# Two layers of a gated hybrid backbone: first tiles, linear attention and mLSTM reordered for TensorE's neighbours, and attention's logits in runs of four

## The chip, the cores and the metric

The kernel runs on one core of a Trainium2 chip. The metric is the device time of one execution in microseconds (us). The kernel before was run three times: 2300.45, 2302.86 and 2303.84 us, so its median is 2302.86. Engines are named as the profile names them: PE is TensorE (PEld its weight loads), DVE is VectorE, ACT is ScalarE, POOL is GpSimd and SP is SyncE.

## What is computed

There are 256 latent tokens and 256 context tokens of width 1024, and two layers. Every sub-layer is an RMS norm with a shift, scale and gate that a conditioning vector sets.

```python
def trunk_layer(x, ctx, c, c_ctx, cos, sin, lp, last):
    ...
    x = x + 0.5 * mod_l[:, 2] * swiglu(adaln(x, mod_l, 0, g[0]), lp['ffn1_w13'], lp['ffn1_w2'])
    ...
    y_l, y_c = token_mixer(adaln(x, mod_l, 1, g[1]), adaln(ctx, mod_c, 1, g[1]), cos, sin, lp, not last)
    x = x + mod_l[:, 5] * y_l
    x = x + 0.5 * mod_l[:, 8] * swiglu(adaln(x, mod_l, 2, g[2]), lp['ffn2_w13'], lp['ffn2_w2'])
```

The token mixer runs three branches over one input projection: windowed attention (8 query heads, 2 key heads of 64 channels, RMS norms of queries and keys, rope for latent tokens, a sink in the softmax; context tokens see context only, latent ones a window and the context), a bidirectional gated linear attention (4 heads, keys 64 wide, values 128) and a bidirectional mLSTM (4 heads of 128). Each branch is multiplied by a sigmoid gate (`s_a`, `s_g`, `s_m`) of the projection and by an output matrix; the sum goes through `w_o`. The last layer gives latent tokens only.

## The kernel before, in words

**Layout and dense products.** Activations are held with channels on the 128 partitions and tokens along the free axis: 512 columns in layer 0, context first. In layer 1's mixer, queries and what follows from them are needed for the 256 latent tokens alone (`c0=256`), keys and values for all. Every large product is split into a high and a low part: `mm3` (L258 to L260) issues three matmuls per 128x128 block of weights (hi with hi, lo with hi, hi with lo), so a dense tile of 128 channels is 24 matmuls into one PSUM tile of the pool `acc`. Weights come by DMA as `raw`; ACT makes the high part (L224, 128x1024), DVE the low one (L225). These dense matmuls are most of what PE does.

**PSUM and order.** PSUM has two pools of four tiles, `acc` for dense tiles and `mx` for everything else. The program is written in one order; a scheduler of the framework turns it into one instruction list per engine, and each engine takes its list strictly in order. A tile of a pool is given out in program order.

**The start** (`start`). The eight tiles of `x` come by DMA; ACT squares them, and PE sums the squares of the first five over the channels with `ones_d` (L356, through the helper line L340), DVE adds the other three (L361) and PE sums that. `partial(k)` is the product of the conditioning vector with block k of the modulation weights (L401), `vectors(k)` turns it into columns, `norm(k)` applies norm, scale and shift to channel block k (L628 to L630: `t`, `xh`, `xl`), and `unit(u, k)` is the three matmuls of dense tile u with block k. The order here is written out by hand and kept with `seq`.

**Linear attention** (`gla`, twice per layer, `ft` 0 and 1). Each call makes gate sums on ACT and DVE, transposes decayed keys (`t` of L782, PE L785), forms chunk states (L795) and attention within chunks. `fill()` issues the next half of a dense tile of `gr`, or a part of `mv`; there are 16 such steps in a layer, and calls beyond that do nothing.

**mLSTM** (`mlstm`, twice per layer for two heads each). `bcast` (L957 to L961) spreads one row of a table over all partitions: a 128x128 matmul with a one-hot column of `sel`, once for the high and once for the low part. It is called for two directions and two heads, three times each. `den1` (L1017) and `qn` (L1023, L1025) collect the denominators in bands of 32 columns. `head_norm` (L727) closes each head.

**Attention.** Keys and four query tiles go through `qk_norm` (L1062 to L1070): a copy, a square on ACT, a sum over 64 channels on PE (L1067), Ln, Exp and a square on ACT (L575, L576, L578), three steps on DVE; the tables of ACT are loaded anew after each first square (L143). `rope` (L1072 to L1079) turns the latent columns. `attention` then loops over two halves `a` and the blocks of 128 queries: `weights` makes four logit tiles (L1123, 64 channels deep, `kv` 0 and 1 on the two halves of the rows), mask, maximum, exponential and sum; `fills()` issues one dense tile (two in layer 1) of the gate `sa`, of which there are eight; then `values` of the step before transposes the weights in blocks of 128 keys (L1147) and multiplies them with the values (L1154, 64 columns wide).

## Time and profile before

| | |
|---|---|
| median of three runs | 2302.86 us |
| the profiled execution | 2299.65 us |
| its span | 2297.5 us |
| mean granted clock of PE | 0.998 |
| PE busy | 2269.5 us, 99% |
| DVE, ACT busy | 1532.1 us (67%), 970.8 us (42%) |
| DMA | 314.94 MB, mean 137 GB/s |

The 2.15 us between span and time are launch and end. A busy share is a mean over stages; PE's waits stand as single entries in a list, with the instruction that ended each. The stages lie as follows (us from the span's start): start to 57, first FFN of layer 0 to 427, its linear attention to 575, a stretch of dense work to 610, mLSTM to 735, attention with its norms to 862, branches and output to 1003, second FFN to 1365; the same for layer 1 with the first FFN to 1743, linear attention to 1853, mLSTM to 1957, norms to 1988, attention to 2040, output to 2100, and the last FFN to the end.

### The profile page before, as it was taken

The numbers are of one execution on the slowest core, as the hardware profiler recorded it, in microseconds if no ns is written. First come the engines' busy times: TensorE is split into PE (matmuls) and PEld (weight loads), VectorE is DVE, ScalarE is ACT, GpSimd is POOL, SyncE is SP. The second block draws the span as 40 slices with busy tenths as digits, with TensorE's granted clock in tenths as the row PEclk, the third lists the DMA queues.
The fourth block names the chain that finished last, engine by engine and source line by source line (L and its number), as shares of the span: only waits on it lengthen the run. The fifth ranks groups of instructions, "written<-read, shape, count | busy, mean of one in ns | idle before, by whom it ended". The sixth has DMA issues, their size and how long they took to land.

```text
span 2297.5 us, 32871 instructions
## 1 busy us (share of the span) xinstructions
PE 2269.5 (99%) x12494; PEld 1890.6 (82%) x12494; DVE 1532.1 (67%) x3214; ACT 970.8 (42%) x1566; POOL 53.7 (2%) x65
## 2 busy tenths in 40 slices
PE   8999999999999999999999999999999999999999
PEld 4888888877877668888888898888888788889999
DVE  5786875689766763768733357855547897876755
ACT  4322224556545642352222253222246665745443
POOL 0000001000000000200000010000010000001000
PEclk9999999999999999999999999999999999999999
DMA  7655554221212113435532236655433333335764
GB/s 281 220 199 162 193 179 143 92 60 56 83 55 66 63 46 92 156 120 189 172 116 92 83 117 207 200 162 193 152 124 96 90 113 98 125 118 190 233 199 147
DMA packets 140430, 314.94 MB, mean 137 GB/s; under 512 B 30192, under 2 KB 41328, under 8 KB 140144
## 3 DMA queue, kind: packets, MB, share of 16 engines
q1 hardware_dynamic: 139248, 309.69, 41.7%
q0 software_dynamic: 1024, 3.15, 0.4%
q8 instruction: 98, 1.61, 0.3%
q14 instruction: 60, 0.49, 0.1%
HBM read 308.59 MB, written 4.19 MB: 136 GB/s over the span
## 4 chain that ended last, share of the span: by engine, by line
PE 72%; DVE 4%; ACT 2%; DMA 1%; issue 1%; SPq 0%; DVEq 0%; ACTq 0%
PE acc L258 21%; PE acc L259 21%; PE acc L260 20%; PE mx L1123 1%; PE mx L1154 1%; PE mx L1147 1%; DVE lo L225 1%; DMA f<-in_modt_dram 1%; PE mx L1057 1%; PE mx L814 1%; PE mx L988 1%; PE mx L727 1%; PE mx L960 0%; PE mx L1017 0%; PE acc L302 0%
## 5 line engine op out<-in xcount | busy, mean ns | idle before, releaser
L224 ACT CAST hi<-raw 128x1024 fp32r<-128x1024 f32 (+2 forms) x445 | 433.8, 977 | 962.9 <-PE acc L259 623.2
L258 PE MATMUL acc<-xh,hi 128*128 128x512 f32 (+1 forms) x2184 | 779.9, 357 | 5.6 <-ACT xh L629 5.3
L259 PE MATMUL acc<-xl,hi 128*128 128x512 f32 (+1 forms) x2184 | 779.2, 357 | 0.2
L260 PE MATMUL acc<-xh,lo 128*128 128x512 f32 (+1 forms) x2184 | 776.0, 355 | 0.6 <-DVE lo L225 0.6
L225 DVE TENSOR_TENSOR lo<-raw,hi 128x1024 fp32r<-128x1024 f32 (+2 forms) x445 | 502.5, 1132 | 311.1 <-ACT hi L224 302.5
L258 PEld LDWEIGHTS acc<-xh,hi 128*128 128x128 f32 x2184 | 413.5, 189 | 70.8 <-issue 7.0
L259 PEld LDWEIGHTS acc<-xl,hi 128*128 128x128 f32 x2184 | 413.5, 189 | 64.7 <-issue 8.0
L260 PEld LDWEIGHTS acc<-xh,lo 128*128 128x128 f32 x2184 | 413.6, 189 | 62.9 <-issue 5.8
L260 PE MATMUL acc<-f,lo 128*128 128x512 f32 (+1 forms) x896 | 313.7, 350 | 0.0
L258 PE MATMUL acc<-f,hi 128*128 128x512 f32 (+1 forms) x896 | 313.4, 350 | 0.0
L514 DVE SCALAR_TENSOR_TENSOR u<-f,f 128x512 f32<-128x512 f32 x448 | 284.7, 686 | 14.0 <-DMA f<-in_modt_dram 14.0
L259 PE MATMUL acc<-t,hi 128*128 128x512 f32 (+1 forms) x704 | 248.2, 353 | 0.0
L258 PEld LDWEIGHTS acc<-f,hi 128*128 128x128 f32 x896 | 169.4, 189 | 23.2 <-issue 1.2
L260 PEld LDWEIGHTS acc<-f,lo 128*128 128x128 f32 x896 | 169.5, 189 | 22.1 <-issue 0.4
L650 DVE TENSOR_TENSOR t<-t,acc 128x512 f32<-128x512 f32 (+1 forms) x89 | 54.2, 609 | 151.5 <-PE acc L260 150.1
L259 PEld LDWEIGHTS acc<-t,hi 128*128 128x128 f32 x704 | 133.1, 189 | 18.2
L638 DVE SCALAR_TENSOR_TENSOR x<-acc,ggt,x 128x256 f32<-128x256 f32 x136 | 61.2, 480 | 88.1 <-PE acc L260 87.9
L592 POOL TENSOR_TENSOR t<-t,t 128x256 f32<-128x256 f32 x45 | 44.8, 1013 | 1121.4 <-ACT t L588 1121.4
L259 PE MATMUL acc<-x,hi 128*128 128x512 f32 (+1 forms) x192 | 65.3, 342 | 0.0
L314 ACT CAST f<-t 128x512 fp32r<-128x512 f32 (+1 forms) x92 | 51.5, 559 | 20.9 <-DVE t L650 19.2
L629 ACT ACTIVATE xh<-t,mod 128x256 fp32r<-128x256 f32 x88 | 39.3, 500 | 44.2 <-DVE t L628 44.2
L315 DVE TENSOR_TENSOR t<-t,f 128x512 fp32r<-128x512 f32 (+1 forms) x90 | 54.7, 607 | 2.4 <-ACT f L314 2.4
(311 smaller groups left out, 2464.6 us busy)
## 6 DMA issues: line engine op xcount, KB each, us to landing
raw<-in_w_dram SPq DMA_DIRECT2D x179, 512.0 KB, 3.6
f<-in_modt_dram SPq DMA_DIRECT2D x256, 256.0 KB, 4.7
raw<-in_win_dram SPq DMA_DIRECT2D x110, 512.0 KB, 3.5
raw<-in_w_dram SPq DMA_DIRECT2D x61, 384.0 KB, 3.1
raw<-in_w_dram SPq DMA_DIRECT2D x61, 320.0 KB, 2.8
raw<-in_wout_dram SPq DMA_DIRECT2D x16, 512.0 KB, 3.5
raw<-in_wo_dram SPq DMA_DIRECT2D x16, 512.0 KB, 4.0
f<-in_modw_dram SPq DMA_DIRECT2D x16, 256.0 KB, 6.2
```

Source lines behind the costliest of these rows:

```text
L224: a = A.copy(hi[:, :n], raw[:, :n])
L225: b = V.tensor_tensor(lo[:, :n], raw[:, :n], hi[:, :n].bitcast(F32), ALU.subtract)
L258: mm(o, wh, xh[:, cs], start=first, stop=False)
L259: mm(o, wh, xl[:, cs], start=False, stop=False)
L260: mm(o, wl, xh[:, cs], start=False, stop=last)
L314: A.copy(hi[:, cs], src[:, cs])
L315: tt(lo[:, cs], src[:, cs], hi[:, cs].bitcast(F32), ALU.subtract)
L514: V.scalar_tensor_tensor(junk[:], raw[:], 1.0, cond[s][h][:], ALU.mult, ALU.mult, accum_out=part[:, k, s, h:h + 1])
L592: G.tensor_tensor(sums[c.start][0][:, c], sums[c.start][0][:, c], q[:, c], ALU.add)
L629: a = act(xh[:, c], t[:, c], AF.Identity, bias=sh[:, k, s:s + 1])
L638: V.scalar_tensor_tensor(X[m][:, c], ps[:, c], gate[:, m, s:s + 1], X[m][:, c], ALU.mult, ALU.add)
L650: tt(t[:, c], t[:, c], pb[:, c], ALU.mult)
```

## The change

`start`: PE sums all eight squares. The second modulation product stands ahead of the first unit, the second norm and the third product come earlier among the units.

`gla`: one call of `fill()` is added for `ft == 0`, ahead of the loop that forms the decayed keys.

`bcast`: two directions are spread in one call, each with a matmul of 32 rows by 128 columns at its own band of rows, first both high parts, then both low ones. The callers' loops follow, and the four `den1` are written ahead of `qn`.

`attention.weights`: the four logits are written ahead of the softmax, the two of `b=0` in pool `mx`, the two of `b=1` in pool `acc`. `attention.values`: the product of a key block is written behind the transposes of the next one.

```diff
@@ start
             i = seq("ACT", act(q[:], X[k][:], AF.Square))
-            if k < 5:
-                pe(ms[:], ones_d[:], q[:], k == 0, False)
-            elif k == 5:
-                total = q
-            else:
-                tt(total[:], total[:], q[:], ALU.add)
-        pe(ms[:], ones_d[:], total[:], False, True)
+            pe(ms[:], ones_d[:], q[:], k == 0, k == KD - 1)
...
+        partial(1)
         unit(0, 0)
-        partial(1)
-        unit(1, 0)
         vectors(1)
         norm(1)
+        unit(1, 0)
+        partial(2)
         unit(0, 1)
-        partial(2)
+        vectors(2)
         unit(1, 1)
-        vectors(2)
         cast(2, 0)
         norm(2)
@@ gla
         act(ends[:, 2:4, :], ends[:, 0:2, :], AF.Exp, scale=1.0 / 16)
+        if ft == 0:
+            fill()
@@ bcast
-    def bcast(r, hi, lo, cs):
-        ps = mx()
-        s = sel[:, r:r + 1].to_broadcast([128, 128])
-        mm(ps[:, cs], s, hi[:, cs], True, False)
-        mm(ps[:, cs], s, lo[:, cs], False, True)
-        return ps
+    def bcast(rs, hi, lo, cs):
+        out = [mx() for _ in rs]
+        for n, x in enumerate((hi, lo)):
+            for ps, r in zip(out, rs):
+                rows = slice(32 * (r // 2), 32 * (r // 2) + 32)
+                mm(ps[:, cs], sel[rows, r:r + 1].to_broadcast([32, 128]), x[rows, cs], n == 0, n == 1)
+        return out
@@ mlstm
-            for d in range(2):
-                r = 2 * (2 * d + hl) + hp
-                ab = bcast(r, R["ah"], R["al"], cs)
+            for d, ab in enumerate(bcast([2 * (2 * d + hl) + hp for d in range(2)], R["ah"], R["al"], cs)):
...
                 mm(den1[rr, cs], onec[:] if hp == 0 else onec2[:], sw[d, hl][:, cs], True, True)
+        for hl in range(2):
+            for d in range(2):
+                q = 2 * d + hl
+                rr = slice(32 * q, 32 * q + 32)
                 for c in range(q0, 4):
...
-            for d in range(2):
-                r = 2 * (2 * d + hl) + hp
-                rb = bcast(r, rh, rl, cs)
+            rs = [2 * (2 * d + hl) + hp for d in range(2)]
+            for d, rb in enumerate(bcast(rs, rh, rl, cs)):
                 tt(sw[d, hl][:, cs], sw[d, hl][:, cs], rb[:, cs], ALU.mult)
-                wb = bcast(r, wh, wl, cs)
+            for wb in bcast(rs, wh, wl, cs):
                 e = W()
@@ attention.weights
+            pss = {}
             for b in range(2):
                 for kv in range(2):
-                    h, j = 4 * kv + 2 * a + b, 2 * kv + b
                     r = slice(64 * kv, 64 * kv + 64)
-                    ps = mx()
+                    ps = pss[b, kv] = (mx, acc)[b]()
                     mm(ps[:, 0:nk], aq[2 * a + b][r, qc], kh[r, 0:nk], True, True)
+            for b in range(2):
+                for kv in range(2):
+                    h, j, ps = 4 * kv + 2 * a + b, 2 * kv + b, pss[b, kv]
                     if lat:
@@ attention.values
             po = mx()
+            def product(kb, t):
+                for kv in range(2):
+                    mm(po[64 * kv:64 * kv + 64, 0:256], vt[:, kb * 128 + 64 * kv:kb * 128 + 64 * kv + 64],
+                       t[:, 256 * kv:256 * kv + 256], kb == 0, kb == nb - 1)
+            due = None
             for kb in range(nb):
...
-                for kv in range(2):
-                    mm(po[64 * kv:64 * kv + 64, 0:256], vt[:, kb * 128 + 64 * kv:kb * 128 + 64 * kv + 64],
-                       t[:, 256 * kv:256 * kv + 256], kb == 0, kb == nb - 1)
+                if due:
+                    product(*due)
+                due = kb, t
+            product(*due)
```

The order of instructions moves in more places than the diff names. Three of them, on PE; `mx` and `acc` are PSUM tiles, the first number is the tile's.

The start, from the three spare matmuls with `ones_d` on: `acc57` and `acc58` are the first two dense tiles, `mx68` is the second modulation product. Before:

```order
L340 MATMUL acc2_123<-u3_124,ones_d_97 128x512 x2
L340 MATMUL mx63_254<-ct_93,u62_246 128x2 x2
L340 MATMUL acc2_123<-u3_124,ones_d_97 128x512
L340 MATMUL acc57_233<-xh41_217,f36_201 128x512
L340 MATMUL acc57_233<-xh41_217,f37_202 128x512
L340 MATMUL acc57_233<-xl42_218,f36_201 128x512
L401 MATMUL mx68_275<-y26_181,ccs_96 32x256 x2
L401 MATMUL mx68_275<-y27_182,ccs_96 32x256 x2
L401 MATMUL mx68_275<-y28_183,ccs_96 32x256 x2
L401 MATMUL mx68_275<-y29_184,ccs_96 32x256 x2
L340 MATMUL acc58_234<-xh41_217,f64_260 128x512
L340 MATMUL acc58_234<-xh41_217,f65_261 128x512
```

After:

```order
L340 MATMUL acc2_123<-u3_124,ones_d_97 128x512 x2
L340 MATMUL mx63_254<-ct_93,u62_246 128x2 x2
L340 MATMUL acc2_123<-u3_124,ones_d_97 128x512
L395 MATMUL mx68_272<-y26_181,ccs_96 32x256 x2
L395 MATMUL mx68_272<-y27_182,ccs_96 32x256 x2
L395 MATMUL mx68_272<-y28_183,ccs_96 32x256 x2
L395 MATMUL mx68_272<-y29_184,ccs_96 32x256 x2
L340 MATMUL acc57_233<-xh41_217,f36_201 128x512
L340 MATMUL acc57_233<-xh41_217,f37_202 128x512
L340 MATMUL acc57_233<-xl42_218,f36_201 128x512
L340 MATMUL mx70_286<-ct_93,u69_281 128x2 x2
L340 MATMUL acc58_234<-xh41_217,f64_260 128x512
```

The four matmul pairs of `mx68` stand ahead of the first unit in place of behind it, and the second unit (`acc58`) behind `mx70`, the vectors of the second block.

A step of layer 0's attention: L1123 and L1122 are logits, L1147 and L1156 transposes, L1154 and L1149 products with the values. Before, with dense matmuls between the step's first four transposes and these rows:

```order
L1154 MATMUL mx1468_6790<-t1470_6796,f1372_6397 64x256 x2
L1147 MATMUL mx1471_6800<-ct_93,t1440_6661 128x128
L1147 MATMUL mx1471_6800<-ct_93,t1444_6673 128x128
L1147 MATMUL mx1471_6800<-ct_93,t1442_6667 128x128
L1147 MATMUL mx1471_6800<-ct_93,t1446_6679 128x128
L1123 MATMUL mx1476_6814<-f1373_6399,f1382_6446 128x512
L1154 MATMUL mx1468_6790<-t1472_6805,f1372_6397 64x256 x2
L1123 MATMUL mx1478_6821<-f1373_6399,f1382_6446 128x512
L1123 MATMUL mx1480_6828<-f1373_6399,f1391_6493 128x512
L1123 MATMUL mx1482_6835<-f1373_6399,f1391_6493 128x512
L259 MATMUL acc1488_6857<-xl806_3393,hi1486_6853 128x512
```

After:

```order
L1156 MATMUL mx1469_6791<-ct_93,t1446_6679 128x128
L1156 MATMUL mx1471_6798<-ct_93,t1443_6667 128x128
L1156 MATMUL mx1471_6798<-ct_93,t1445_6675 128x128
L1156 MATMUL mx1471_6798<-ct_93,t1444_6671 128x128
L1156 MATMUL mx1471_6798<-ct_93,t1446_6679 128x128
L1122 MATMUL acc1478_6818<-f1373_6399,f1391_6493 128x512
L1122 MATMUL acc1479_6820<-f1373_6399,f1391_6493 128x512
L1149 MATMUL mx1468_6790<-t1470_6796,f1372_6397 64x256 x2
L1149 MATMUL mx1468_6790<-t1472_6803,f1372_6397 64x256 x2
L1122 MATMUL mx1476_6814<-f1373_6399,f1382_6446 128x512
L1122 MATMUL mx1477_6816<-f1373_6399,f1382_6446 128x512
L258 MATMUL acc1488_6857<-xh795_3382,hi1486_6853 128x512
```

One and three logits with a product between have become two and two, with both products between them; the eight transposes stand in one run.

Layer 1's last query norm to the first logits: L1067 and L1066 are the sum over channels of a norm, L1075 and L1074 the rope, `acc3707` the fourth of the eight `sa` gate tiles, `acc3681` the first. Before:

```order
L258 MATMUL acc3707_17614<-xh3025_14294,hi3705_17610 128x256
L259 MATMUL acc3707_17614<-xl3026_14295,hi3705_17610 128x256
L260 MATMUL acc3707_17614<-xh3025_14294,lo3706_17611 128x256
L1067 MATMUL mx3641_17368<-t3640_17364,ct_93 128x256
L1075 MATMUL mx3652_17394<-f3603_17175,ct_93 128x256
L1075 MATMUL mx3654_17400<-f3612_17222,ct_93 128x256
L1075 MATMUL mx3656_17406<-f3621_17269,ct_93 128x256
L258 MATMUL acc3707_17614<-xh3027_14296,hi3705_17610 128x256
L259 MATMUL acc3707_17614<-xl3028_14297,hi3705_17610 128x256
L260 MATMUL acc3707_17614<-xh3027_14296,lo3706_17611 128x256
L258 MATMUL acc3707_17614<-xh3029_14298,hi3705_17610 128x256
```

After:

```order
L1066 MATMUL mx3641_17368<-t3640_17364,ct_93 128x256
L1074 MATMUL mx3652_17394<-f3603_17175,ct_93 128x256
L1074 MATMUL mx3654_17400<-f3612_17222,ct_93 128x256
L1074 MATMUL mx3656_17406<-f3621_17269,ct_93 128x256
L1074 MATMUL mx3658_17412<-f3630_17316,ct_93 128x256
L1074 MATMUL mx3660_17418<-f3639_17363,ct_93 128x256
L1122 MATMUL mx3669_17433<-f3603_17175,f3612_17222 128x512
L1122 MATMUL mx3670_17435<-f3603_17175,f3612_17222 128x512
L1122 MATMUL acc3671_17437<-f3603_17175,f3621_17269 128x512
L1122 MATMUL acc3672_17439<-f3603_17175,f3621_17269 128x512
L258 MATMUL acc3681_17476<-xh3025_14294,hi3679_17472 128x256
```

Before, dense matmuls of the `sa` tiles stand between the norms' sums and between ropes and logits. After, the sums of all four query norms stand in a row ahead of the ropes (the other three directly ahead of these rows), the logits follow the ropes, and the first `sa` tile follows the logits. From the last head norm of mLSTM (L727) to the first logits, PE's list holds 16 dense matmuls, the sum of the key norm, 25 dense matmuls, and then these rows.

## Rows read from the trace of the kernel before

**Rows 1.** The page, part 1: busy us, share of the span, instructions.
```profile
PE 2269.5 (99%) x12494; PEld 1890.6 (82%) x12494; DVE 1532.1 (67%) x3214; ACT 970.8 (42%) x1566; POOL 53.7 (2%) x65
```

**Rows 2.** PE's waits over the span: us in total, times, longest.
```profile
PE acc L258 <- ACT xh L629: 5.3, 2, 4.1
PE mx L785 <- DVE t L782: 3.4, 3, 1.6
```

**Rows 3.** Timeline, PE, the start: start us, us, instruction, [idle before].
```profile
13.00 1.12 PE L340 MATMUL mx<-t,ones_d 128*128 128x512 f32 x2 [1.54 <-DVE t L361]
...
20.30 0.73 PE L340 MATMUL acc<-xh,f 128*128 128x512 f32 x2 [1.01 <-ACT xh L629]
...
21.25 1.07 PE L401 MATMUL mx<-y,ccs 128*32 128x256 f32 x16
...
25.54 0.74 PE L340 MATMUL acc<-xh,f 128*128 128x512 f32 x2 [1.98 <-ACT xh L629]
```

**Rows 4.** Busy time by stretch (PE, PEld, DVE, ACT), layer 0.
```profile
455.00:506.00 51.00, 47.97 (x325) 36.70 (x325) 40.10 (x78) 24.40 (x37) 0.00 (x0) 1.00 0.20 61
...
772.00:862.00 90.00, 89.84 (x446) 56.69 (x445) 61.69 (x183) 41.74 (x105) 0.00 (x0) 1.00 0.15 47
```

**Rows 5.** Timeline, PE, two broadcasts of layer 1's mLSTM (lines 960, 961).
```profile
1950.48 0.28 PE L960 MATMUL mx<-t,sel 128*128 128x256 f32 x1
1950.60 0.28 PE L961 MATMUL mx<-t,sel 128*128 128x256 f32 x1
```

**Rows 6.** Timeline, PE, one logit of 256 keys between dense matmuls.
```profile
777.73 0.40 PE L260 MATMUL acc<-xh,lo 128*128 128x512 f32 x1
778.06 0.70 PE L1123 MATMUL mx<-f,f 64*128 64x256 f32 x2
778.68 0.50 PE L258 MATMUL acc<-xh,hi 128*128 128x512 f32 x1
```

**Rows 7.** Timeline, PE, logits of 512 keys, one step of layer 0.
```profile
786.54 1.12 PE L1123 MATMUL mx<-f,f 64*128 64x512 f32 x2
787.59 0.65 PE L1154 MATMUL mx<-t,f 128*64 128x256 f32 x4
788.18 2.19 PE L1123 MATMUL mx<-f,f 64*128 64x512 f32 x6
790.29 0.50 PE L259 MATMUL acc<-xl,hi 128*128 128x512 f32 x1
```

**Rows 8.** Timeline, PE, layer 0's first logits and first transposes of weights.
```profile
772.86 0.87 PE L1123 MATMUL mx<-f,f 64*128 64x256 f32 x4
...
783.22 0.27 PE L1147 MATMUL mx<-ct,t 128*128 128x128 f32 x1
```

**Rows 9.** Window, PE on `acc`, from last head norm to first logits, layer 1.
```profile
1956.63:1988.69 32.06, 28.69 (x214) 1.00 0.44 136
```

**Rows 10.** Timeline, PE, layer 1's first logits.
```profile
1988.69 2.66 PE L1123 MATMUL mx<-f,f 64*128 64x512 f32 x8
```

**Rows 11.** Timeline, ACT, one query norm of layer 1.
```profile
1964.10 0.41 ACT L1065 ACTIVATE t<-f 128x256 f32<-128x256 f32 x1
1964.41 1.03 ACT L224 CAST hi<-raw 128x1024 fp32r<-128x1024 f32 x1
1965.45 1.28 ACT L143 ACT_TABLE_LOAD   x1
1966.75 0.47 ACT L575 ACTIVATE t<-mx,kc 128x256 f32<-128x256 f32 x1
...
1968.96 0.41 ACT L1065 ACTIVATE t<-f 128x256 f32<-128x256 f32 x1
```

**Rows 12.** Timeline, PE, its longest wait.
```profile
2100.26 0.58 PE L258 MATMUL acc<-xh,hi 128*128 128x256 f32 x1 [4.10 <-ACT xh L629]
```

**Rows 13.** Windows around it: PE, PEld, DVE, ACT, POOL busy, then PEclk.
```profile
2099.20:2100.20 1.00, 0.00 (x0) 0.00 (x0) 1.00 (x3) 0.50 (x2) 0.00 (x0) 0.50 0.00 0
2100.20:2105.90 5.70, 5.64 (x25) 5.50 (x26) 5.49 (x14) 3.56 (x9) 0.00 (x0) 0.50 0.00 0
```


## The prediction

> **What bounds the kernel now.** I read the page first: TensorE is busy for 99% of the span [rows 1], so a microsecond is won only by giving PE less to do or by taking away one of its few waits, and it is lost wherever PE finds its next instruction not ready. Then the list of what PE waited for: the largest entries are one wait of 4.1 us for `xh` of L629 and, in the linear attention, VectorE's `t` of L782 (three times, 3.4 us in all) [rows 2]. Third, PE's timeline and the load of VectorE at the places that the diff touches: the first tiles, linear attention, mLSTM's broadcasts, the logits [rows 3 to 8]. Fourth, because PE takes its instructions in order, I followed in the order of both kernels what PE has to do while it is waiting for another engine. That led to layer 1's query and key norms [rows 9 to 11], which no line of the diff names.
>
> The profiled execution took 2299.65 us, 3.21 us less than the median of the runs shown (2302.86). The sum is made as a difference and added to either. A measurement here can tell about 0.2%, 4.6 us, from no change.
>
> **The start.** PE waits 1.01 us for the first normed tile and 1.98 us for the second [rows 3], with a third, shorter wait behind. The changed order puts the second modulation product, which takes 1.07 us on PE [rows 3], into the first of these waits; the vectors and the norm that follow from it come as much earlier, so the second wait shrinks too. I take -2.8 us; with every wait gone it would be -3.8, and -1.5 if the later weights' casts are then what PE waits for. That PE sums all eight squares I cost at nothing: it waits 1.54 us for VectorE's sum of the last three [rows 3], and of the three sums that take the place of one, two fit there; the last square, and so its load, ends the chain either way.
>
> **Linear attention.** One `fill` (half a dense tile) is put where PE waits for `t`, 3.4 us over both layers [rows 2]. The number of steps stays, so the last step is missing later. In layer 0 VectorE is busy 40.1 of 51 us [rows 4], and what is filled early is partly waited for later. I take -1.5 us for both layers; bounds -3.4 (all of it gone) and +1 (PE late for VectorE's next step).
>
> **mLSTM's broadcasts.** Before, each is two 128-row matmuls like the dense ones around them, 0.12 us apart at 256 columns [rows 5]: no change of tile shape. After, two directions run in two bands of 32 rows. What a change of shape costs I read at a lone logit of 64 rows between dense 512-column matmuls: it starts at 778.06 where 777.73 + 0.23 was due, and the dense one after it starts at 778.68, itself late [rows 6]; beside its own two 0.21 us halves that is 0.3 to 0.4 us for going there and back. The nearest row for bands is a pair of logits, which takes as long as one (below). So a run of four broadcasts costs 2 x 0.12 + 0.39 = 0.63 us in layer 1 against 0.48 to 0.65 now, 0.84 against 0.91 in layer 0; but the scheduler splits many of them into runs of two, which save one matmul and pay the same two changes. Counted over the runs of the new order: +0.2 us in layer 0, +1.8 in layer 1. I take +2; bounds -1 (changes hidden) and +4 (bands not overlapped). The Trainium skill, "TensorEngine Tiling (Array Packing)", Key Properties, says that a change of tiling mode drains TensorE, which speaks against this part; by it alone the runs of two would all lose, and the rows 6 agree with it.
>
> **Attention's runs, layer 0.** One logit of 512 columns between others takes 1.05 us (786.54 to 787.59) and three take 2.11 (788.18 to 790.29) [rows 7]: two on different halves of the rows cost as one. Before, 1 + 3 stand in a step, 3.16 us; now 2 + 2, 2.1. With both products in one run a step of the latent queries falls by 1.3 us, four times; the two steps of 256-column logits with four key blocks rise by 1.3 each, because product, transposes and logits now alternate, at the price of rows 6 for each pair of changes; the first eight logits, which stood nearly singly, gain 2. Sum -3.5. Against it: the first values' transposes now come only 24 dense matmuls (5.4 us) behind the last logits, where 10.4 us lay between first logit and first transpose before [rows 8], and VectorE is busy 61.7 of 90 us [rows 4]. I take 2 us of new waits there: -1.5; bounds -3.5 and +4.
>
> **Attention's runs, layer 1.** Four logits already stand together once [rows 10], two groups not; the same products in fours, and 48 dense between the groups: -2 us; bounds -3 and 0.
>
> **Layer 1's norms, the largest term.** The logits of half `b=1` now take `acc` buffers, and these are given out in the order of the program: the `sa` gate tiles of the fill come behind them. In the new order all eight stand after layer 1's first logits. Before, 214 dense matmuls lie between the last head norm and the first logits, 32.06 us [rows 9], 25.7 of it dense at 0.12; after, 16 + 25 = 41, or 4.9 us. In layer 0 the first logits are of context tokens and need no rope, so there a gate tile still covers. What PE must wait for is ScalarE: each norm is a square, a table load of 1.28, Ln (0.47), Exp and a second square (much like the first, 0.41) [rows 11]. From one norm's square to the next's is 4.86 us (1964.10 to 1968.96), with two weight casts in it, that is 2.9 to 3.0 without. In the new order ScalarE has two casts in the key's norm (512 wide, 5.8 us), two small ones (L314), each about as long as a square, in each of the next two (3.5 each), none in the last two (3.0 each): 18.8. Ahead of it stand the head norm's own Ln, Exp and square with the hand-over, some 2.0, behind it three VectorE steps and a rope, each taken at 0.4: 1.7: first logits 22.5 us after the head norm. PE's own work there, at the prices of before, is 4.9 + (32.06 - 25.7) = 11.3. The other 173 dense are not lost, they run elsewhere; the stretch costs 22.5 - 11.3 = +11 us; bounds +8 (no gaps at hand-overs) and +14 (0.3 us at each).
>
> **The clock.** Within the 4.10 us wait before 2100.26 the granted clock falls to half, 1.2 GHz, and stays there until 2105.9; 25 dense matmuls take 5.7 us in place of 3.0 [rows 12, 13]. In the new stretch PE is idle more than half of 22 us, with five waits of about 3 us each. I take one fall: +3; bounds 0 and +5 (logits at half clock too). The Trainium skill, "TensorE: Matmul & The Clock Gate", Part 1, has the low clock as the default that activity lifts; the fall in rows 13 agrees.
>
> **Sum:** -2.8 - 1.5 + 2 - 1.5 - 2 + 11 + 3 = +8.2 us: 2307.9 for the profiled execution, 2311 for the median.
>
> **Rivals.**
> (a) The clock holds, since single norm matmuls fall between the waits: +5.2, 2308. For it: no wait would be as long as 4.10.
> (b) VectorE becomes the bound in layer 0's attention: +4 in place of -1.5, so +13.7, 2316.6. For it: its share there; against: 28 us are free.
> (c) No measurable change: ScalarE's chain at its lower bound (+8), the clock holds, no new waits in layer 0, bands at +1: -2.8 - 1.5 + 1 - 3.5 - 2 + 8 = -0.8, 2302.
> (d) Faster: the chain isn't what PE waits for. The terms other than chain and clock make -5.8; the kernel is faster by over 0.2% if the first logits of layer 1 follow the head norm within 12.6 us in place of 22.5, that is if a norm takes 1.1 us where ScalarE's steps add up to 3.0. With table loads overlapped, about -6, 2297. Rows 11 speak against it.
>
> **Numbers.** The forecast as summed 0.44, (a) 0.20, (b) 0.12, (c) 0.15, (d) 0.09. (a) lies at the 0.2% line, half on each side: slower 0.44 + 0.12 + 0.10 = 0.66, same 0.25, faster 0.09. The range runs from (c) with linear attention's waits all gone, 2300, to (b) with the clock's upper bound, 2319.
>
> **What would show it.** In layer 1 PE's waits for ScalarE or VectorE between head norm and first logits add up to 10 us or more, the first logits come about 22 us after the head norm, and the granted clock falls beside them. At the start the first FFN tiles come nearly 3 us earlier. A latent step's tiled work in layer 0 is near 4.2 us. I am wrong if PE's waits in layer 1's norms stay under 5 us, or if layer 0's attention takes over 92 us.

## The result, and the profile after

| | before | after |
|---|---|---|
| median of four runs | 2302.15 us | 2322.18 us |
| lowest to highest | 2300.45 to 2303.84 | 2317.44 to 2322.97 |
| the profiled execution, its span | 2299.65, 2297.5 | 2322.97, 2321.2 |
| mean granted clock of PE | 0.998 | 0.993 |

The changed kernel takes 1.0089 [1.0076, 1.0101] of the time before: 20.0 us slower by the medians. The forecast was 2311 with a range to 2319: the right side, less than half of the size, and the measured time lies above the range.

In part 1 of the page of the kernel after, PE is busy for 98% of the span and that is 14.4 us more than in [rows 1], part of it matmuls at half clock:

```profile
PE 2283.9 (98%) x12498; PEld 1887.7 (81%) x12498; DVE 1529.5 (66%) x3212; ACT 972.2 (42%) x1568; POOL 53.4 (2%) x65
```

The list of what PE waited for, after (us in total, times, longest); beside the wait for `xh` that was there before [rows 2], entries that are new, or longer than before, head it:

```profile
PE mx L1066 <- ACT t L1064: 8.4, 4, 2.6
PE acc L258 <- ACT xh L623: 5.3, 2, 4.1
...
PE acc L258 <- ACT t L1132: 2.6, 1, 2.6
...
PE mx L1149 <- DVE t L1159: 2.0, 5, 0.7
PE acc L260 <- DVE lo L225: 1.8, 1, 1.8
...
PE acc L1122 <- ACT f L1273: 0.9, 1, 0.9
```

To see where the loss arises I took the last dense matmul of each stage in PE's list (the same product of the same weights in both kernels) and subtracted its start before from its start after. The steps between these differences are what each stage costs:

```
stage                             us lost   so far
start                               -3.1     -3.1
layer 0: FFN, linear attention      -0.2     -3.2
layer 0: mLSTM                      +0.4     -2.8
layer 0: norms and attention        +4.8     +2.0
layer 1: linear attention           +3.4     +5.5
layer 1: mLSTM                      +1.8     +7.3
layer 1: norms and attention       +15.1    +22.4
rest                                +1.3    +23.7
```

These are two profiled executions. That of before was 2.5 us under its median (the last section has a likely reason) and that of after 0.8 over, so 23.7 answers to the 20.0 of the medians.

**The start.** PE's timeline after (start us, us, instruction, [idle before]). The second modulation product now stands at 19.15, inside what was the 1.01 us wait of [rows 3]; the 1.98 us wait is 0.17:

```profile
19.15 1.07 PE L395 MATMUL mx<-y,ccs 128*32 128x256 f32 x16
...
24.28 0.73 PE L340 MATMUL acc<-xh,f 128*128 128x512 f32 x2 [0.17 <-ACT xh L623]
```

**Layer 0's attention.** The same view. Where [rows 8] had four pairs of first logits at 772.86 and then dense work, PE now waits twice: logits in `acc` for a gate tile's tanh to free a buffer (0.92), and a gate tile for an exponential (2.56):

```profile
771.03 0.70 PE L1122 MATMUL acc<-f,f 64*128 64x256 f32 x2 [0.92 <-ACT f L1273]
771.38 1.36 PE L1122 MATMUL mx<-f,f 64*128 64x256 f32 x4
775.31 0.50 PE L258 MATMUL acc<-xh,hi 128*128 128x512 f32 x1 [2.56 <-ACT t L1132]
```

A latent step of 512 keys further on answers to [rows 7]: logits two and two, each pair some 1.05 us from start to next start, the eight transposes in one run, and a wait of 0.24 for the copies of the transposed weights:

```profile
782.51 1.03 PE L1156 MATMUL mx<-ct,t 128*128 128x128 f32 x8
783.47 1.13 PE L1122 MATMUL acc<-f,f 64*128 64x512 f32 x4
784.55 0.65 PE L1149 MATMUL mx<-t,f 128*64 128x256 f32 x4
785.43 0.65 PE L1149 MATMUL mx<-t,f 128*64 128x256 f32 x4 [0.24 <-DVE t L1159]
786.02 1.13 PE L1122 MATMUL mx<-f,f 64*128 64x512 f32 x4
```

And a step of 256-column logits with four key blocks, where products, transposes and then logits alternate:

```profile
805.31 0.65 PE L1149 MATMUL mx<-t,f 128*64 128x256 f32 x4
805.90 0.66 PE L1156 MATMUL mx<-ct,t 128*128 128x128 f32 x4
806.63 0.65 PE L1149 MATMUL mx<-t,f 128*64 128x256 f32 x4
```

**Layer 1's norms**, the stretch that answers to [rows 9, 10], from the last head norm (L721) to the first logits (L1122):

```profile
1968.37 0.70 PE L721 MATMUL mx<-t,ones_h 128*128 128x256 f32 x2
...
1976.58 0.70 PE L1066 MATMUL mx<-t,ct 128*128 128x256 f32 x2 [1.41 <-ACT t L1064]
1979.89 0.70 PE L1066 MATMUL mx<-t,ct 128*128 128x256 f32 x2 [2.61 <-ACT t L1064]
1983.20 1.22 PE L1066 MATMUL mx<-t,ct 128*128 128x256 f32 x2 [2.61 <-ACT t L1064]
1986.19 1.22 PE L1066 MATMUL mx<-t,ct 128*128 128x256 f32 x2 [1.77 <-ACT t L1064]
...
1990.83 1.22 PE L1074 MATMUL mx<-f,ct 128*128 128x256 f32 x2 [0.85 <-DVE t L1076]
1992.55 1.22 PE L1074 MATMUL mx<-f,ct 128*128 128x256 f32 x2 [0.50 <-DVE f L1068]
1993.70 2.08 PE L1122 MATMUL mx<-f,f 64*128 64x512 f32 x4
1995.57 1.92 PE L1122 MATMUL acc<-f,f 64*128 64x512 f32 x4
```

The same norm matmul lasts 0.70 us before 1980 and 1.22 after. Windows of the kernel after (the number behind the five engines is the granted clock) name the places where it fell to half, of which before had only one, that of [rows 13]:

```profile
776.00:779.50 3.50, 3.50 (x10) 2.72 (x9) 2.81 (x11) 1.72 (x9) 0.00 (x0) 0.56 0.00 0
1813.00:1817.00 4.00, 4.00 (x11) 2.90 (x10) 3.35 (x6) 2.24 (x3) 0.00 (x0) 0.57 0.01 5
1981.00:1997.00 16.00, 10.67 (x22) 5.22 (x22) 10.63 (x29) 7.62 (x16) 0.00 (x0) 0.50 0.00 1
2120.00:2126.00 6.00, 3.33 (x14) 3.19 (x15) 5.26 (x14) 3.07 (x8) 0.00 (x0) 0.54 0.00 0
```

### The profile page after: what moved, and what is told of

The parts are those of the page before. It is cut to its first block, busy times and chain, and to the rows that moved or that the text cites. A ratio compares the mean times of both kernels' runs of the same rounds, so it can differ in the third digit from the quotient of the medians.

```text
span 2321.2 us, 32881 instructions
## 1 busy us (share of the span) xinstructions
PE 2283.9 (98%) x12498; PEld 1887.7 (81%) x12498; DVE 1529.5 (66%) x3212; ACT 972.2 (42%) x1568; POOL 53.4 (2%) x65
## 4 chain that ended last, share of the span: by engine, by line
PE 87%; DVE 7%; ACT 3%; DMA 2%; issue 1%; SPq 0%; DVEq 0%; ACTq 0%
PE acc L258 25%; PE acc L259 25%; PE acc L260 25%; DVE lo L225 1%; DMA f<-in_modt_dram 1%; PE mx L810 1%; PE mx L1149 1%; ACT hi L224 1%; PE acc L340 1%; PE mx L959 1%; PE mx L340 1%; PE mx L1056 1%; PE mx L721 1%; PE mx L986 1%; PE mx L1156 0%
## 5 line engine op out<-in xcount | busy, mean ns | idle before, releaser
L225 DVE TENSOR_TENSOR lo<-raw,hi 128x1024 fp32r<-128x1024 f32 (+2 forms) x445 | 502.3, 1131 | 326.6 <-ACT hi L224 317.9
```

What stands on the lines that cost most here:

```text
L225: b = V.tensor_tensor(lo[:, :n], raw[:, :n], hi[:, :n].bitcast(F32), ALU.subtract)
```

## The experiments

The theory after this view: most of the loss is the order in which the tiles of `acc` are given out. Dense matmuls cover the other engines' chains: PE works on them while ScalarE and VectorE prepare what PE needs next. Logits that take `acc` tiles stand ahead of the gate tiles of the fill, so the dense matmuls that were this cover come behind the chains. The rivals: a cost of TensorE itself (bands of 32 rows, changes of tile shape), and the late product of the values. Each run below has the kernel before beside it on its own chip; differences are of medians.

### The four parts alone

`e1_start`, the kernel before with the new `start` alone:

```diff
...
+        partial(1)
         unit(0, 0)
-        partial(1)
-        unit(1, 0)
         vectors(1)
         norm(1)
+        unit(1, 0)
...
```

> The kernel before with the new start alone. Theory (each part acts where it stands, and the stages after the start only shift): dense work begins 3.1 us earlier, as in the changed kernel's trace, and nothing later gives it back: 2302.15 - 3.1 = about 2299. Rival (what is won at the start is lost again at the 4.1 us wait before the last FFN or at the weights' loads): within 1 us of the kernel before.

Measured: 2295.59 against 2300.60, 0.998 [0.9971, 0.999].

`e2_gla`, the kernel before with the added call in the linear attention:

```diff
+        if ft == 0:
+            fill()
```

> The kernel before with the additional fill in the linear attention alone. Theory: the step that is filled early is missing later and cuts the runs of small matmuls into more pieces: layer 0 about -0.2 us, layer 1 about +3, so +3 in all. Rival (the loss of 3.4 us that the changed kernel shows in layer 1's linear attention comes from the other parts): -1 to -3 us, since one of the two 1.5 us waits goes.

Measured: 2305.34, 1.0022 [1.0012, 1.0031].

`e3_mlstm`, the kernel before with the new `bcast` and the callers' loops:

```diff
-    def bcast(r, hi, lo, cs):
+    def bcast(rs, hi, lo, cs):
...
+                rows = slice(32 * (r // 2), 32 * (r // 2) + 32)
+                mm(ps[:, cs], sel[rows, r:r + 1].to_broadcast([32, 128]), x[rows, cs], n == 0, n == 1)
```

> The kernel before with the broadcasts in bands of 32 rows and the reordered mLSTM alone. Theory: changes of tile shape cost more than the overlap of two bands gives: +2.5 us (+0.4 in layer 0, +2 in layer 1). Rival: the loss seen there in the changed kernel comes of dense work that attention's order moved into this stage: 0 or less.

Measured: 2303.87, 1.0011 [1.0002, 1.0021].

`e4_att`, the kernel before with the new `weights` and `values`:

```diff
...
-                    ps = mx()
+                    ps = pss[b, kv] = (mx, acc)[b]()
...
+                if due:
+                    product(*due)
+                due = kb, t
+            product(*due)
```

> The kernel before with the new attention alone. Theory: this part carries nearly all of the loss, +4.8 us in layer 0 and +14 to +15 in layer 1 with a fall of the granted clock after the last head norm, and +1 behind it: +20, 2322. Rival (the idle stretch in layer 1 needs mLSTM's new order too): under +10.

Measured: 2317.50, 1.0076 [1.0061, 1.0091].

The four differences are -5.0, +4.7, +3.3 and +16.9, together +19.9, where the whole change is +20.0. By the medians the combination has no cost of its own, though by the intervals of these five ratios one of up to some 6 us (an estimate) could hide in the sum. Stage by stage the parts do not add up so well: layer 1's linear attention loses 1.8 in `e2_gla` and 3.4 in the whole change (a fall of the clock, last section), its mLSTM 3.8 in `e3_mlstm` and 1.8 in the whole, which is not explained here. The start gains nearly twice what was forecast; the other three lose, and the attention loses most. Against the theories of these runs, `e1_start` gains 1.9 us more, `e2_gla` loses 1.7 more, `e3_mlstm` 0.8 more and `e4_att` 3.1 less; none of the four rivals holds.

### The pool of the logits

`e5_l1mx` is the changed kernel with the logits of layer 1 in `mx`, `e6_allmx` with all of them:

```diff
-                    ps = pss[b, kv] = (mx, acc)[b]()
+                    ps = pss[b, kv] = (mx, mx if c0 else acc)[b]()
```

```diff
-                    ps = pss[b, kv] = (mx, acc)[b]()
+                    ps = pss[b, kv] = mx()
```

> The changed kernel with one edit: in layer 1 all four logits go to the pool mx, in layer 0 they stay as changed. Theory (the acc buffers of layer 1's logits are what keeps the sa gate tiles behind them, and so PE idle and its clock low in the norms): the waits for the norms' squares and the fall of the clock after the last head norm go, about -14 us against the changed kernel, 2307. Rival (the idle stretch comes from mLSTM's new order or from the run of four itself): no more than -4, 2317 or more.

> The changed kernel with all logits in mx, in both layers. Theory (in layer 0 the 0.9 and 2.6 us waits come of logits and gate tiles that wait for each other's acc buffers): against the run with mx in layer 1 alone another -3 to -5 us, 2302 to 2304, and no fall of the clock in layer 0's attention. Rival (the waits are VectorE's and ScalarE's load): within 1.5 us of the run with mx in layer 1 alone.

Measured against 2300.71: `e5_l1mx` 2313.62, 1.0057 [1.0042, 1.0072]; `e6_allmx` 2308.69, 1.0039 [1.0025, 1.0054]. In layer 1's norms and attention the stage costs +5.65 in `e5_l1mx` where the whole change has +15.1: that pool alone is worth 9.5 us there in the profiles. By the medians, +20.0 and +12.9, it is 7.1 in all, between the theory's 14 and the rival's 4. All that is left of PE's waits between 1960 and 2000 in `e5_l1mx`:

```profile
PE acc L258 <- ACT f L1273: 1.2, 1, 1.2
```

A wait of 0.6 for the rope follows at the first logits, which come at 2002 in this run. But +5.65 is more than I gave what stays. The next runs look for it. In layer 0 the stage falls from +4.8 to +2.4 with `mx`; the entries for L1132 and for the gate's tanh (L1273) are gone from this stretch in `e6_allmx`, whose only wait there is (PE's waits, 735 to 870):

```profile
PE mx L1149 <- ACT t L1161: 1.1, 1, 1.1
```

The median of `e6_allmx` is 4.9 us under that of `e5_l1mx`, its span only 2.4; its profiled execution was the longest of its five.

### The halves of the attention's change

`e9_values`, the kernel before with only the later product; `e10_logits`, with only the logits in runs and the old products:

```diff
...
-                for kv in range(2):
-                    mm(po[64 * kv:64 * kv + 64, 0:256], vt[:, kb * 128 + 64 * kv:kb * 128 + 64 * kv + 64],
-                       t[:, 256 * kv:256 * kv + 256], kb == 0, kb == nb - 1)
+                if due:
+                    product(*due)
+                due = kb, t
+            product(*due)
```

```diff
...
-                    ps = mx()
+                    ps = pss[b, kv] = (mx, acc)[b]()
...
```

> The kernel before with the later product of the key blocks alone, logits as before. Theory (with four key blocks the later product breaks one long run into alternating pieces): +2.4 us in layer 0 and about +5.6 in layer 1, so +8, 2308 to 2309. Rival (what is left in layer 1 with all logits in mx comes of dense work that mLSTM took there): +3 or less.

> The kernel before with the logits in runs of four alone, half of them in acc, products as before. Theory: the norms of layer 1 are left without dense work, +9.5 us there, and the waits for acc buffers in layer 0 give +2.4: about +12, 2312 to 2313, with the clock's fall in layer 1. Rival (the runs of four pay once the product isn't moved): +6 or less.

Measured against 2300.40: `e9_values` 2305.09, 1.0021 [1.0012, 1.003]; `e10_logits` 2313.98, 1.0064 [1.0049, 1.0079]. By stage, the halves and both together (`e4_att`):

```
                              values   logits   both
layer 0: norms, attention      +2.3     +2.6    +4.8
layer 1: norms, attention      +1.5    +10.6   +12.8
```

They add up within 0.7 us. The chain of norms in layer 1 belongs to the logits in `acc` alone: `e10_logits` has the waits, in the same place (PE's waits, 1955 to 2000):

```profile
PE mx L1067 <- ACT t L1065: 6.3, 3, 2.6
PE mx L1075 <- DVE f L1069: 1.0, 1, 1.0
...
```

The later product is a loss in both layers. In layer 0 it is what this run's theory had; in layer 1 it is +1.5 where the theory had +5.6, so the run ends between theory and rival. With four key blocks it alternates with transposes (the rows at 805.31 above), and layer 1 has latent queries alone, whose products all run over four key blocks.

### Bands of 32 rows, or the order

`e7_mrows128` is `e3_mlstm` with the broadcasts on all 128 rows again, in the new order of the loops:

```diff
-                rows = slice(32 * (r // 2), 32 * (r // 2) + 32)
-                mm(ps[:, cs], sel[rows, r:r + 1].to_broadcast([32, 128]), x[rows, cs], n == 0, n == 1)
+                mm(ps[:, cs], sel[:, r:r + 1].to_broadcast([128, 128]), x[:, cs], n == 0, n == 1)
```

> The kernel before with the reordered mLSTM, but each broadcast with all 128 rows again. Theory (the bands' changes of tile shape are the loss): within 1 us of the kernel before, 2.5 us less than with bands. Rival (the order of hi, hi, lo, lo and of den1 ahead of qn is the loss): +2.5 to +3.5 us as with bands.

Measured: 2298.62, 0.9991 [0.9981, 1.0]. Against `e3_mlstm` (+3.3) this is 5.4 us less. PE's list has the same 12494 matmuls, by the names of their tiles, in the same order in both kernels, so the loss is the tile shape. Whether the new order by itself gains isn't shown: -2.1 has an interval that reaches no change. A run of two broadcasts between dense matmuls in `e3_mlstm`, PE's timeline:

```profile
1958.74 0.28 PE L259 MATMUL acc<-xl,hi 128*128 128x256 f32 x1
1958.95 0.49 PE L963 MATMUL mx<-t,sel 32*128 32x256 f32 x2
1959.37 0.38 PE L260 MATMUL acc<-xh,lo 128*128 128x256 f32 x1
1959.60 0.28 PE L258 MATMUL acc<-xh,hi 128*128 128x256 f32 x1
```

and the same run in `e7_mrows128`:

```profile
1953.37 0.28 PE L259 MATMUL acc<-xl,hi 128*128 128x256 f32 x1
1953.48 0.40 PE L962 MATMUL mx<-t,sel 128*128 128x256 f32 x2
1953.72 0.28 PE L260 MATMUL acc<-xh,lo 128*128 128x256 f32 x1
1953.84 0.28 PE L258 MATMUL acc<-xh,hi 128*128 128x256 f32 x1
```

From the first dense matmul to the last it is 0.86 us in bands and 0.47 on 128 rows: 0.39 more, the price of a change there and back that [rows 6] gave. The Trainium skill, "TensorEngine Tiling (Array Packing)", Key Properties, has a change of tiling mode drain the engine; these two fences agree, and put 0.39 us on it, while bands with four matmuls in a run (0.43 us from 1956.99 to 1957.42 in `e3_mlstm`) took no longer than two (0.42).

### The fill, by layer

Linear attention was the part that I had called a small gain. `e13_fill_l0` adds the call in layer 0 only, `e14_fill_l1` in layer 1 only:

```diff
+        if ft == 0 and c0 == 0:
+            fill()
```

```diff
+        if ft == 0 and c0:
+            fill()
```

> The kernel before with the additional fill in layer 0's linear attention alone. Theory (layer 1's order is what the fill harms): layer 1 as before, layer 0 at -0.2: within 1 us of the kernel before. Rival (the fill costs at both places): +2 us or more.

> The kernel before with the additional fill in layer 1's linear attention alone. Theory: all of the loss, +4 to +5.5 us, about 2 of it in the linear attention and 3 to 4 behind it, where 48 dense matmuls that lay between the key norm and the first logits now stand ahead of them. Rival (only the linear attention itself loses): +2 us or less.

Measured against 2300.89: `e13_fill_l0` 2300.22, 1.0002 [0.9992, 1.0011]; `e14_fill_l1` 2305.52, 1.002 [1.001, 1.003]. All of it is layer 1, and only 1.8 us of it lies in the linear attention: 3.8 come more than 100 us later, in the norms and the attention. The gate tiles of that stretch have moved up too: between the last head norm and the first logits PE has 157 dense matmuls, where [rows 9] had 214. PE's waits of `e14_fill_l1` from 1870 to 2060 begin:

```profile
PE mx L1069 <- ACT t L1067: 1.7, 1, 1.7
PE acc L258 <- ACT f L1265: 1.5, 1, 1.5
```

So behind the linear attention the fill loses by the mechanism of the logits: dense work spent early is missing where ScalarE's chain has to be covered. How much may be missing shows beside it: the order of `e3_mlstm` and `e7_mrows128` leaves 188 dense matmuls there, and that stage loses nothing in either.

Inside layer 1's linear attention the fill does not do what it was put there for. The wait for `t` stays, 1.6 us before and 1.5 now (PE's waits, 1743 to 1880, of before and of `e14_fill_l1`):

```profile
PE mx L785 <- DVE t L782: 1.9, 2, 1.6
PE mx L787 <- DVE t L784: 1.5, 1, 1.5
```

And the small matmuls of the stage stand in 33 runs between dense ones in place of 28. Five more changes there and back at the 0.39 us above are 2 us, an estimate; the stage loses 1.8. In layer 0 that wait does shrink, from 1.5 to 0.3 (`e13_fill_l0`), but other waits grow and the runs go from 28 to 30: the stage gains 0.2.

In norms and attention of layer 1, `e5_l1mx` still lost 5.65, and the fill (3.8) and the later product (1.5) together are 5.3. That leaves no gain of the runs in `mx`, as in layer 0, where `e6_allmx` loses 2.4 and the later product alone 2.3. The division of the 5.65 is argued from these sums, not shown: `e5_l1mx` has 213 dense matmuls between head norm and first logits and waits of only 1.8 us.

### Cover for the norms

`e11_early4` is the changed kernel with four gate tiles written ahead of layer 1's attention, to lay dense work back beside the norms:

```diff
+        if c0:
+            for _ in range(4):
+                fill()
         ao = attention(...)
```

> The changed kernel with four of layer 1's eight sa gate tiles issued ahead of its attention, logits still half in acc. Theory (not the pool matters but the place of the gate tiles behind the first logits): waits for the norms' squares go, no fall of the clock there, -9 us against the changed kernel, about 2312. Rival (the dense work is then missing between the runs of the softmax): less than -4.

Measured: 2316.75, 1.0073 [1.0056, 1.009], 3.7 us less than the whole change. The rival holds: the waits of the norms shrink from 8.4 us to one of 3.4, but the ropes still wait (1.4 and 0.9), the clock still falls (0.69 from 1990 to 1995), and the tiles are then missing between the softmaxes, where a new wait stands (PE's waits, 1955 to 2060):

```profile
PE mx L1066 <- ACT t L1064: 3.4, 1, 3.4
PE acc L258 <- ACT t L1132: 1.6, 1, 1.6
...
```

Eight tiles do not cover both chains when they are cut into whole tiles in this order. How finer pieces would do wasn't tried.

### The parts that pay

`e8_best` keeps the new start, and of the attention's change what paid in layer 0: `acc` for the logits of the latent queries there, and the later product only where two key blocks stand. `e12_best3` adds the mLSTM of `e7_mrows128`:

```diff
...
-                    ps = mx()
+                    ps = pss[b, kv] = (mx, acc if lat and not c0 else mx)[b]()
...
+                if nb > 2:
+                    product(kb, t)
+                    continue
+                if due:
+                    product(*due)
+                due = kb, t
+            if due:
+                product(*due)
```

> The kernel before with the new start, and in layer 0's attention the b=1 logits in acc for the latent queries alone and the later product for the two key blocks of the context queries alone; layer 1, linear attention and mLSTM as before. Theory: the start gives -5 as it did alone, four steps of layer 0 fall by about 1 us each: 2291 to 2293. Rival (the acc buffers make new waits here as well): no better than the new start alone, 2295.6 or more.

> The best version so far (new start, layer 0's latent logits half in acc, later product for two key blocks) with the reordered mLSTM at 128 rows. Theory (parts add up): -2 against it, 2291. Rival (the -2 of the 128-row order alone was the spread of the start): no better than 2293.

Measured: `e8_best` 2293.17 against 2300.71, 0.9969 [0.9958, 0.998]; `e12_best3` 2292.29 against 2300.40, 0.9967 [0.9954, 0.998]. Layer 0's attention gains 2.5 us in both profiles: the runs of four do pay where nothing takes their buffers and nothing alternates. Both kernels beat before and after; they cannot be told from each other, so the -2.1 of `e7_mrows128` did not come again clear of noise. PE's busy time in `e12_best3` is 2266.7 us, 2.8 under [rows 1], and the rest of its gain is idle time.

## Why the prediction was right in its sign and wrong in its size

Two terms failed, and each left its own bounds: the fill in linear attention (-1.5 forecast, bounds -3.4 and +1, measured +4.7) and attention's runs in layer 0 (-1.5 forecast, bounds -3.5 and +4, measured +4.8).

**The start, -2.8.** Right in the profile (-3.1). The medians have -5.0, probably since at the old start the clock also falls in many executions; that is in the last section.

**Layer 1's norms, +11, with the clock, +3.** Right in mechanism and size. The first logits came 25.3 us after the head norm (1968.37 to 1993.70), forecast 22.5 with the clock apart, with 41 dense matmuls between them as forecast. Less the 11.3 of PE's own work that is +14.0, as 11 + 3. ScalarE's chain from the key norm's square to the last norm's last step took 18.4 us (1970.39 to 1988.82 in its timeline), forecast 18.8. PE's waits there are 8.4 + 0.85 + 0.50 = 9.75 us, just under the 10 that I had set as the mark. The clock stayed at half for 16 us, and the ropes and the first logits fell into it: eight logits took 2.08 + 1.92 us as they stand above, against 2.66 in [rows 10]. But the text gave all of it to the logits in `acc`, and these alone leave 74 dense matmuls (`e4_att`, `e10_logits`) and cost 9.5 to 10.6 us in the profiles (the whole change less `e5_l1mx`, and `e10_logits`). The fill and mLSTM's order take the other 33. Rival (d) is excluded by the four waits.

**Linear attention, -1.5 for both layers.** Wrong; this is the first step that failed. The term took waits away and priced nothing for it. Layer 0 is 0 (`e13_fill_l0`), layer 1 +4.6 (`e14_fill_l1`): the 1.5 us wait there stayed, the small matmuls were cut into five more runs, and the dense work that went into the fill was missing in layer 1's norms, where the 214 matmuls of [rows 9] became 157. The text said that what is filled early "is partly waited for later" and put no place to it. In the whole change that last loss does not come on top, as the 41 dense matmuls of the norms' term were counted in the whole new order; there the two stages of linear attention cost -0.2 + 3.4 = +3.2, with 1.5 of it a fall of the clock.

**Attention's runs in layer 0, -1.5.** Wrong, the second step that failed: +4.8. The four entries of the sum (four times -1.3, twice +1.3, and -2) make -4.6, not the -3.5 that it says; with them the term is -2.6 and the whole forecast +7.1, further off. By the starts of the same dense matmuls in both kernels, the four steps of 512 keys gained 3.0 us in all, 5.2 forecast: their tiled work is 4.6 to 5.0 us, with waits of 0.24 to 0.69 for the copies, where 4.2 was the sign to look for. The two steps with four key blocks lost 2.5, 2.6 forecast. The first eight logits lost 2.5 where a gain of 2 was forecast: logits and gate tiles share the four buffers of `acc` and each waits for the other, 0.92 and 2.56 us. I had looked at this sharing in layer 1 alone and written that in layer 0 "a gate tile still covers". The last product lost 1.3, and the clock at half from 776 to 779.5 cost 1.6. By the mark that I had set, over 92 us, the stretch is past it: 4.8 more than the 90 of [rows 4].

**Attention's runs in layer 1, -2.** Not seen. In `mx` the runs gained nothing that shows; in `acc` they come with the norms' waits and were not measured apart. The later product, which this term took for free, lost 1.5 (`e9_values`). So that norms, clock and runs, 12 together, came near the +12.8 of `e4_att` is partly luck.

**mLSTM's broadcasts, +2.** Right: +3.3, within -1 to +4, by the price per change of shape that [rows 6] gave. The bands cost 5.4 us at the same order (`e7_mrows128`); whether the order gives 2.1 of it back is not clear of noise.

**The rest, +1.3.** Not foreseen: at 2176.65 PE waits 1.80 us for a weight's low part, which VectorE makes (the entry for L225 in the list; before, 0.6). It was not tested by itself, and `e13_fill_l0`, whose median is that of the kernel before, has the same wait of 1.8 us in its profile.

**The range** ended at 2319, with rival (b), VectorE as the bound in layer 0, and the clock's upper bound. VectorE was not the bound: the waits there are for ScalarE's exponential and tanh and, in steps below 0.7 us, for VectorE's copies. The upper bounds of all terms add up to +26.5, 2329; the range left out that several could be wrong at once. By the parts alone the sum reads so:

```
                         forecast   measured alone
start                      -2.8         -5.0
linear attention           -1.5         +4.7
mLSTM                      +2.0         +3.3
attention, norms, clock   +10.5        +16.9
sum                        +8.2        +19.9
```

Of the 11.7 us between the sums, 6.2 are the fill and 6.3 the attention of layer 0; the others nearly cancel. Much of both has one reason, as I read it: I followed in PE's list what an edit moves where the largest term stood, and priced the other places from single waits and single rows.

## What to carry to other kernels

Where dense tiles cover the chains of other engines, they are one budget for the whole stage list: a `fill` added early, or a tile that takes a buffer of the fill's pool, has to be followed to the last stretch that the fill covers, counting the dense matmuls left there against the chain's length. A tile shape other than that of its neighbours has to earn the change there and back, 0.39 us here; two small matmuls between dense ones did not. A fill put at a wait is worth the wait only if the wait goes: here it stayed and the fill cut the small matmuls into more runs. Measure the parts of a change alone: here one of four was worth keeping whole, half of another too, and the sum hid both.

## What was not expected of the hardware

**The clock at the start differs between executions of one order.** At the 1.98 us wait of [rows 3] the granted clock held in the profiled execution of before, in `e4_att`, `e10_logits` and `e13_fill_l0`, and fell in those of `e2_gla`, `e3_mlstm`, `e7_mrows128`, `e9_values` and `e14_fill_l1`, which all have the old start. In `e2_gla`, a window (the clock is 0.75 in it, and 0.50 in the 5 us behind it) and then PE's timeline after that wait (1.58 us in place of the 1.07 of [rows 3], and a pair of units at 1.22 in place of 0.73):

```profile
25.00:30.00 5.00, 3.87 (x22) 2.16 (x23) 1.84 (x5) 1.94 (x4) 0.00 (x0) 0.75 1.05 387
```

```profile
26.13 0.73 PE L340 MATMUL acc<-xh,f 128*128 128x512 f32 x2 [1.98 <-ACT xh L629]
...
27.08 1.58 PE L401 MATMUL mx<-f,ccs 128*32 128x256 f32 x16
28.59 1.22 PE L340 MATMUL acc<-xh,f 128*128 128x512 f32 x2
```

None of the seven profiles with the new start (the changed kernel, `e1_start`, `e5_l1mx`, `e6_allmx`, `e8_best`, `e11_early4`, `e12_best3`) has it; `e1_start` in this window:

```profile
25.00:30.00 5.00, 4.82 (x19) 3.00 (x20) 4.27 (x12) 3.03 (x7) 0.00 (x0) 1.00 1.05 385
```

So the gain of the new start is the wait and, in part of the executions, the fall behind it. That fits -5.0 in the medians beside -3.1 in the profiles, where that of before has no fall there, and before's profiled execution lying under its median. Of the other executions only the mean clock of the whole is known (0.996 to 0.999 for the kernel before), which does not tell where it fell, so this much stays an inference.

**A fall without a wait.** At 1813 in the changed kernel the clock goes to half (the second of the windows above) though PE had no wait there (busy for 4.00 of 4.00 us in that window): two gate matmuls of 32 rows ran just before, over a microsecond each. PE's timeline:

```profile
1810.83 1.12 PE L733 MATMUL mx<-f,gw 32*128 32x512 f32 x2
1811.88 0.51 PE L304 MATMUL acc<-lo,xh 128*128 128x512 f32 x1
1812.32 1.12 PE L733 MATMUL mx<-f,gw 32*128 32x512 f32 x2
1813.37 0.79 PE L302 MATMUL acc<-hi,xh 128*128 128x512 f32 x1
```

It costs some 1.5 us: layer 1's linear attention loses 3.4 with it, and 1.8 in the two runs below that lack it. `e5_l1mx`, `e6_allmx` and `e11_early4` have it too; `e2_gla` and `e14_fill_l1`, which have the fill too and run the same matmuls there, do not. The Trainium skill, "TensorE: Matmul & The Clock Gate", Part 1, has the clock follow how busy PE has been; the falls at 776 and 1981 came behind waits and agree, while in this one PE is busy for all of the window. What sets it off in these four kernels and not in the two others stays open.
